# Up projections of three feed-forward layers as seven block products in place of eight, in a one-core backbone kernel

## The chip, the cores and the metric

The kernel runs on one core of a Trainium2 chip. The metric is device time in microseconds from start to end of one launch. The host lays data out, the core does all arithmetic. The engines are named as the profile names them: PE (TensorE, matmuls; PEld its weight loads), DVE (VectorE), ACT (ScalarE), POOL (GpSimd), SP (SyncE, which issues most transfers).

## The reference

A backbone of two layers works on 512 tokens (256 context, 256 latent) of width 1024. Each layer is: half-step SwiGLU, a token mixer, half-step SwiGLU; each is modulated by vectors of a conditioning product (w_ada) and wrapped in a LayerNorm.

```python
def swiglu(u, w_up, w_down):
    a, v = jnp.split(u @ w_up, 2, axis=-1)
    return (jax.nn.silu(a) * v) @ w_down

def ffn_sublayer(h, m, j, w_up, w_down, g, b):
    u = modulate(h, m[:, :, 3 * j], m[:, :, 3 * j + 1])
    return post_norm(h, swiglu(u, w_up, w_down), m[:, :, 3 * j + 2], FFN_RES_W, g, b)
```

w_up is 1024 x 5632 (gate half a, value half v), w_down 2816 x 1024. The latent tokens alone are the output, so the second layer's mixer and last feed-forward layer work on 256 columns; the three feed-forward layers before that point work on 512.

## The kernel before

Activations lie with features on the partitions and tokens along the row: u is 8 tiles of 128 x 512 (KT = 8), and half the columns (TL = 256) are context, half latent. All products are made of two parts: a number x is split into hi (x rounded to fp32r, by ACT) and lo (x - hi, by DVE), and `mm3` (L372 to L374) adds hi x hi, hi x lo and lo x hi into a PSUM bank. So each 128 x 128 weight block costs three matmuls.

Weights come in slots of eight blocks (128 x 1024, 512 KB), loaded by SP into one of three raw tiles (`wr`) in a fixed order, the plan. `split_ahead` makes wh (ACT, L342) and wl (DVE, L344) into one of three split slots, as far ahead of PE as slots are free. 

A feed-forward layer `ffn` has an up stage: for each of 22 feature tiles (`ft`), one bank gets the gate (eight blocks over kt), one the value; `act` applies SiLU on ACT (L760), multiplies with the value on DVE (L761), and splits the result into hi (L764) and lo (L765). The first pairs of tiles are begun together, column half by column half, while the LayerNorm of the layer before ends (`k_outer`); in the very first layer three pairs are begun in `ffn_start`. Then the down stage: eight output tiles `m` of 22 blocks each, the last two in column halves (`tail`). After each of them `res_tile` adds it to the residual and POOL sums it up for the LayerNorm (L595 to L599). In the down stage the tiles of u are free, and `more_slots` makes them into three further split slots.

Into both stages the kernel strews `ada_part`: a row block of the conditioning product that later layers need. It loads 128 x 1024 weights through the same raw tiles and makes, on DVE, a multiply-and-sum over 1024 for each of two vectors (L488, twice), then adds a bias (L492).

```python
raw = self.raw_next((("adb", l, j, k),))
for b in range(2):
    nc.vector.scalar_tensor_tensor(self.ada_scr, raw.rearrange("p a b -> p (a b)"), 1.0, self.sb[b],
                                   op0=ALU.mult, op1=ALU.mult, accum_out=o[:, b:b + 1])
```

The instructions on each engine stand in an order that a scheduler makes from the code's order when the kernel is built; each engine runs its own in that order.

## Time and profile before

| | |
|---|---|
| median of 3 runs | 2720.38 us (2718.14 to 2722.66) |
| the profiled execution, its own time | 2722.64 us |
| its span in the trace | 2720.7 us |
| PE busy | 2659.9 us, 98% |
| DVE / ACT / POOL busy | 71% / 45% / 13% |
| mean granted TensorE clock, as a share of full speed | 0.991 |

The busy time of an engine counts an instruction from its start to its end; those of PE overlap, so their pace is read from starts. What the engines do by stage is read from stretches of the trace.

### The profile page before, as it was taken

The page shows a single profiled execution, that of the slowest core. Times are in us where ns is not written, and L with a number is a line of the kernel's source. Part 1 is how long each engine was busy: PE and PEld are TensorE (multiplying, and loading weights), DVE is VectorE, ACT ScalarE, POOL GpSimd, SP SyncE. Part 2 cuts the span into 40 slices and gives each one's busy share as a digit, 9 for nine tenths or more (in the row PEclk, how much of TensorE's full clock was granted, in tenths as well). Part 3 has the DMA queues.
Part 4 walks back from the last instruction along what each step waited for, and adds up shares of the span by engine and source line. Part 5 has one row for each costly group of instructions (what it writes and reads, how often), then busy time and mean ns, then how long its engine had stood idle before and what let it go on. Part 6 is the DMA issues. An engine that isn't in the chain of part 4 may idle for free.

```text
span 2720.7 us, 38673 instructions
## 1 busy us (share of the span) xinstructions
PE 2659.9 (98%) x14869; PEld 2280.2 (84%) x14869; DVE 1928.3 (71%) x3469; ACT 1222.9 (45%) x1755; POOL 353.8 (13%) x296
## 2 busy tenths in 40 slices
PE   9999999999999999999999999999998999999998
PEld 7888897778887888888888888888977898899997
DVE  5788769599877545468887588633697998676654
ACT  4323237963345344433323142332388745574543
POOL 0000132112121000040000130001312112012002
PEclk9999999999999999999999999999999999999999
DMA  7666534134343222235666446532333354343563
GB/s 280 193 189 200 172 122 130 60 99 149 105 134 109 78 86 78 88 99 170 194 195 191 132 129 199 169 120 97 108 123 105 111 174 150 107 142 124 175 191 116
DMA packets 117833, 380.49 MB, mean 140 GB/s; under 512 B 13888, under 2 KB 22352, under 8 KB 117648
## 3 DMA queue, kind: packets, MB, share of 16 engines
q1 hardware_dynamic: 116000, 373.52, 42.5%
q0 software_dynamic: 1504, 4.34, 0.5%
q8 instruction: 116, 1.90, 0.3%
q14 instruction: 69, 0.57, 0.1%
q10 hardware_dynamic: 144, 0.17, 0.0%
HBM read 373.63 MB, written 4.33 MB: 139 GB/s over the span
## 4 chain that ended last, share of the span: by engine, by line
PE 56%; DVE 7%; ACT 3%; issue 2%; DMA 1%; POOL 0%; SPq 0%; POOLq 0%; DVEq 0%; ACTq 0%
PE bank L372 17%; PE bank L373 17%; PE bank L374 17%; PE bank L1282 1%; PE bank L1262 1%; DVE wl L344 1%; DVE x L869 1%; DMA wr<-in_ws_dram 1%; DMA x<-acs_d 1%; DVE f L669 0%; DVE m1l L344 0%; ACT wh L342 0%; PE bank L921 0%; DVE f L670 0%; DVE f L676 0%
## 5 line engine op out<-in xcount | busy, mean ns | idle before, releaser
L342 ACT ACTIVATE wh<-wr 128x1024 fp32r<-128x1024 f32 x388 | 410.2, 1058 | 727.1 <-PE bank L373 493.2
L344 DVE TENSOR_TENSOR wl<-wr,wh 128x1024 fp32r<-128x1024 f32 x388 | 483.6, 1247 | 239.4 <-ACT wh L342 237.6
L488 DVE SCALAR_TENSOR_TENSOR ada_scr<-wr,sb 128x1024 f32<-128x1024 f32 x256 | 316.7, 1237 | 135.9 <-DMA wr<-in_ws_dram 133.2
L372 PE MATMUL bank<-u0h,wh 128*128 128x512 f32 (+1 forms) x660 | 247.1, 376 | 5.5 <-ACT u0h L675 3.8
L372 PE MATMUL bank<-r,wh 128*128 128x512 f32 (+1 forms) x736 | 251.3, 342 | 0.0
L374 PE MATMUL bank<-r,wl 128*128 128x512 f32 (+1 forms) x736 | 249.9, 340 | 0.0
L373 PE MATMUL bank<-r,wh 128*128 128x512 f32 (+1 forms) x736 | 249.7, 340 | 0.0
L374 PE MATMUL bank<-u0h,wl 128*128 128x512 f32 (+1 forms) x660 | 237.2, 360 | 3.9 <-DVE wl L344 3.9
L373 PE MATMUL bank<-u0l,wh 128*128 128x512 f32 (+1 forms) x660 | 236.2, 358 | 2.1 <-DVE u0l L677 2.0
L373 PE MATMUL bank<-u1l,wh 128*128 128x512 f32 (+1 forms) x660 | 235.1, 357 | 0.8 <-DVE u1l L677 0.7
L372 PE MATMUL bank<-u1h,wh 128*128 128x512 f32 (+1 forms) x660 | 233.5, 356 | 0.6 <-ACT u1h L675 0.6
L374 PE MATMUL bank<-u1h,wl 128*128 128x512 f32 (+1 forms) x660 | 234.0, 355 | 0.0
L372 PE MATMUL bank<-u2h,wh 128*128 128x512 f32 (+1 forms) x660 | 233.6, 355 | 0.0
L374 PE MATMUL bank<-u2h,wl 128*128 128x512 f32 (+1 forms) x660 | 233.4, 354 | 0.0
L373 PE MATMUL bank<-u2l,wh 128*128 128x512 f32 (+1 forms) x660 | 233.2, 354 | 0.0
L373 PE MATMUL bank<-u3l,wh 128*128 128x512 f32 (+1 forms) x644 | 228.6, 355 | 1.5 <-DVE u3l L677 1.5
L372 PE MATMUL bank<-u3h,wh 128*128 128x512 f32 (+1 forms) x644 | 228.3, 356 | 0.0
L374 PE MATMUL bank<-u3h,wl 128*128 128x512 f32 (+1 forms) x644 | 228.0, 354 | 0.0
L372 PEld LDWEIGHTS bank<-r,wh 128*128 128x128 f32 x736 | 139.4, 190 | 15.3 <-issue 0.3
L374 PEld LDWEIGHTS bank<-r,wl 128*128 128x128 f32 x736 | 139.5, 190 | 15.1
L373 PEld LDWEIGHTS bank<-r,wh 128*128 128x128 f32 x736 | 139.5, 190 | 14.8
L372 PEld LDWEIGHTS bank<-u0h,wh 128*128 128x128 f32 x660 | 125.6, 191 | 29.7 <-issue 5.6
(530 smaller groups left out, 5919.4 us busy)
## 6 DMA issues: line engine op xcount, KB each, us to landing
wr<-in_ws_dram SPq DMA_DIRECT2D x602, 512.0 KB, 4.0
m1r<-in_ws_dram SPq DMA_DIRECT2D x29, 512.0 KB, 3.9
ada<-in_ws_dram SPq DMA_DIRECT2D x16, 512.0 KB, 9.0
x<-acs_d SPq DMA_DIRECT2D x22, 256.0 KB, 3.4
x<-acs_d SPq DMA_DIRECT2D x39, 128.0 KB, 3.6
x<-in_lw_dram SPq DMA_DIRECT2D x16, 256.0 KB, 3.2
f<-acs_d SPq DMA_DIRECT2D x25, 128.0 KB, 3.4
sb<-s_d SPq DMA_DIRECT2D x6, 512.0 KB, 5.8
```

The source lines that it names most:

```text
L342: self.pin(nc.scalar.activation(hi, raw, AF.Copy))
L344: self.pin(nc.vector.tensor_tensor(lo, raw, hi, op=ALU.subtract))
L372: x = self.pin(nc.tensor.matmul(out, st[0], mv[0], start=start, stop=False, skip_group_check=True))
L373: self.pin(nc.tensor.matmul(out, st[0], mv[1], start=False, stop=False, skip_group_check=True))
L374: self.last_mm = self.pin(nc.tensor.matmul(out, st[1], mv[0], start=False, stop=stop, skip_group_check=True))
L488: nc.vector.scalar_tensor_tensor(self.ada_scr, raw.rearrange("p a b -> p (a b)"), 1.0, self.sb[b], op0=ALU.mult, op1=ALU.mult, accum_out=o ...
L869: nc.vector.scalar_tensor_tensor(ys[:, :, a:z], xs[:, :, a + o:z + o], w(k), ys[:, :, a:z], op0=ALU.mult, op1=ALU.add)
L1262: nc.tensor.matmul(ps[:, 0:256], cc(kt[d], a), vv(a), start=True, stop=True)
L1282: nc.tensor.matmul(cc(po[w], c), lh, rh, start=n == 0, stop=n == len(steps) - 1, skip_group_check=True)
```

## The change

In the three layers with 512 columns, all feature tiles but the first four (five in the first layer) have their gate and value tile computed as one 2 x 2 by 2 x 2 product of quadrants. The weights' quadrants are a11, a12 (the gate's even and odd blocks over kt) and a21, a22 (the value's); the columns' are b11, b12 (even blocks of u, left and right half) and b21, b22 (odd blocks). `products` gives the order of the seven products of a tile p; each is four blocks of 128 x 128 on 256 columns, three matmuls a block. The slots of a tile's seven weight parts are half split slots, so that six parts fit.

- ACT and DVE split each part of 512 on its own (L451, L452) in place of a slot of 1024 at once. The parts of products 7, 6, 5 and 3 are sums of quadrants that POOL makes in place in the raw tiles or in a page (L420).
- `columns` makes the column sums on DVE and splits them, right after the first pairs; `columns_last` replaces one quadrant of u by another sum after the last unchanged tile.
- The outputs are put together from PSUM by copies (ACT) and additions (DVE, L517 to L521). From the ninth tile on v x g stays unsplit (L1027); `late_parts` splits it in the first block of the down stage, into the tiles of the column parts and of u, two results at a time; `move` has POOL copy 16 of these out of u again (L1057, L1061) before u becomes split slots.
- `ada_part(shared=True)` does one of the two sums as a product on POOL (L707), in place, and a sum on ACT (L708). There are two ada parts at a time in the first layer's unchanged tiles, one shared part in each changed tile, and four in a down block where there were two.
- A fourth raw tile is there in the up stage. LayerNorm's preparation moves from the start of the down stage to its sixth block.

```diff
+def products(n):
+    r = []
+    for p in range(n):
+        r += [(p, 1), (p, 7)] + ([(p - 1, 3)] if p else [])
+        r += [(p, m) for m in ((6, 4, 2, 5) if p < n - 1 else (6, 4, 5, 2, 3))]
+    return r
...
+        while len(self.sparts) < len(self.sops):
+            t = self.part_get()
+            if t is None:
+                return False
+            p, m = self.sops[len(self.sparts)]
+            R = self.sraw
+            if m in (1, 7):
+                n = i + 2 * p + (m == 7)
+                R[p, m] = self.raw_next(tuple(self.wlist[8 * n:8 * n + 8])), len(self.seq) - 1
...
+            if m == 1:
+                src = a11
+            elif m == 7:
+                R[p, 5] = self.F()
+                sub(R[p, 5], a21, a22, ALU.add)
+                sub(a21, a11, a21)
+                src = a21
+            elif m == 6:
+                sub(a11, R[p, 5], a11)
+                src = a11
+            elif m == 2:
+                src = a12
+            elif m == 4:
+                src = a22
+            else:
+                src = R[p, m]
+            nc.scalar.activation(flat(t.hi), src, AF.Copy)
+            nc.vector.tensor_tensor(flat(t.lo), src, flat(t.hi), op=ALU.subtract)
+            if m == 2:
+                R[p, 3] = self.F()
+                sub(R[p, 3], a12, a11)
+                self.raw_done(R[p, 1][1])
+            elif m == 4:
+                self.raw_done(R[p, 7][1])
+            elif m in (3, 5):
+                self.fF(src)
+            self.sparts.append(t)
+        self.wn += 2 * self.secs[i]
+        self.raw_less()
+        return True
...
+        for c, (p, m) in enumerate(products(n)):
...
+            X, Z, G, V = x_of[p][:, left], z_of[p], g_of[p], v_of[p]
+            out = Z[:, left] if m in (7, 4) else Z[:, right] if m == 2 else X
+            for b in range(4):
+                if m in (1, 2, 3):
+                    k, s = (2 * b + (m > 1), right if m == 3 else left)
+                    mv = self.uh[k][:, s], self.ul[k][:, s]
+                elif m == 4:
+                    mv = self.uh[2 * b][:, right], self.ul[2 * b][:, right]
+                else:
+                    mv = [x[:, b] for x in self.tparts[{5: 0, 6: 1, 7: 2}[m]]]
+                y = self.mm3(out, (t.hi[:, b], t.lo[:, b]), mv, m in (1, 7) and b == 0, b == 3)
...
+            if m == 1:
+                nc.scalar.activation(G[:, left], X, AF.Copy)
+            elif m == 7:
+                nc.scalar.activation(V[:, right], Z[:, left], AF.Copy)
+            elif m == 6:
+                nc.scalar.activation(V[:, left], X, AF.Copy)
+            elif m == 5:
+                nc.vector.tensor_tensor(V[:, right], X, V[:, right], op=ALU.add)
+            elif m == 4:
+                nc.vector.tensor_tensor(V[:, left], Z[:, left], V[:, left], op=ALU.add)
+            elif m == 2:
+                nc.vector.tensor_tensor(G[:, left], Z[:, right], G[:, left], op=ALU.add)
+                nc.scalar.activation(G[:, left], G[:, left], AF.Silu)
+                self.fB(Z)
+            elif m == 3:
+                nc.scalar.activation(G[:, right], X, AF.Silu)
+                self.fB(x_of[p])
+                finish(fts[p], G, V)
+                self.fF(G, V)
...
+        left, right = HALF
+        b11, b12 = self.ucol[:, :, 0, left], self.ucol[:, :, 0, right]
+        b21, b22 = self.ucol[:, :, 1, left], self.ucol[:, :, 1, right]
+        for o, a, b in ((b11, b12, b11), (b12, b22, b12), (b22, b22, b11), (b21, b21, b22)):
+            nc.vector.tensor_tensor(o, a, b, op=ALU.subtract)
...
+        for n, src in ((2, b12), (1, b22), (0, b11)):
+            hi, lo = self.tparts[n]
+            nc.scalar.activation(hi, src, AF.Copy)
+            nc.vector.tensor_tensor(lo, src, hi, op=ALU.subtract)
...
+        for b in range(KT // 2):
+            src, hi, lo = (x[:, s] for x, s in ((self.ucol[:, b, 1], HALF[0]), (self.uh[2 * b], HALF[1]),
+                                                (self.ul[2 * b], HALF[1])))
+            nc.scalar.activation(hi, src, AF.Copy)
+            nc.vector.tensor_tensor(lo, src, hi, op=ALU.subtract)
...
         nc = self.nc
         for l, j, k in self.ada_q[:n]:
             raw = self.raw_next((("adb", l, j, k),))
             o = self.mods[l][:, j, k, :]
-            for b in range(2):
-                nc.vector.scalar_tensor_tensor(self.ada_scr, raw.rearrange("p a b -> p (a b)"), 1.0, self.sb[b],
-                                               op0=ALU.mult, op1=ALU.mult, accum_out=o[:, b:b + 1])
+            r = raw.rearrange("p a b -> p (a b)")
+            for b in range(1 if shared else 2):
+                nc.vector.scalar_tensor_tensor(self.ada_scr, r, 1.0, self.sb[b], op0=ALU.mult, op1=ALU.mult,
+                                               accum_out=o[:, b:b + 1])
+            if shared:
+                nc.gpsimd.tensor_tensor(r, r, self.sb[1], op=ALU.mult)
+                nc.scalar.activation(r, r, AF.Copy, accum_out=o[:, 1:2])
             self.raw_done()
             c = PR["b_ada"] + j * KT + k
             nc.vector.tensor_scalar(o, o, self.par[l][:, c:c + 1], None, op0=ALU.add)
...
+        reg = 4 + (ps is not None) if paired else NFT
+        sums = ps is not None
+        self.with_u = paired
         ps = ps or self.ffn_begin(l, j, c0)
+        self.with_u = False
...
-        for ft in range(len(ps) // 2, NFT):
+        if paired:
+            self.columns(sums)
+        for ft in range(len(ps) // 2, reg):
             pp = [self.B(), self.B()]
             for i in range(2):
                 for kt in range(KT):
                     w = self.W(("up", l, j, kt, i * NFT + ft))
                     if kt == KT // 2:
-                        self.ada_part()
+                        self.ada_part(1 + sums)
                     self.mm3(pp[i][:, c0:], w, (self.uh[kt][:, c0:], self.ul[kt][:, c0:]), kt == 0, kt == KT - 1)
             act(*pp)
...
+        late = []
+        if paired:
+            self.columns_last()
+            def finish(ft, g, v):
+                if ft < NFULL:
+                    nc.vector.tensor_tensor(g, v, g, op=ALU.mult)
+                    hi, lo = self.R(), self.R()
+                    nc.scalar.activation(hi, g, AF.Copy)
+                    nc.vector.tensor_tensor(lo, g, hi, op=ALU.subtract)
+                    hid.append((hi, lo))
+                else:
+                    nc.vector.tensor_tensor(pages[ft - NFULL], v, g, op=ALU.mult)
+                    hid.append(None)
+                    late.append(ft)
+            def between(p, m):
+                if m == 4:
+                    self.ada_part(shared=True)
+            self.strassen(l, j, range(reg, NFT), finish, between)
...
+        def late_parts(n):
+            for ft in late[:n]:
+                src = pages[ft - NFULL]
+                hi, lo = his.pop(0) if his else spare.pop(0), spare.pop(0)
+                nc.scalar.activation(hi, src, AF.Copy)
+                nc.vector.tensor_tensor(lo, src, hi, op=ALU.subtract)
+                hid[ft] = hi, lo
+            del late[:n]
...
+            for ft in range(NFULL, NFT):
+                if ft >= NFT - 2:
+                    hi = q.tile([P, T], F32R, name=f"hh{l}{jm}_{ft}")
+                    nc.gpsimd.tensor_scalar(hi, hid[ft][0], 1.0, None, op0=ALU.mult)
+                else:
+                    hi = hid[ft][0]
+                lo = q.tile([P, T], F32R, name=f"hl{l}{jm}_{ft}")
+                nc.gpsimd.tensor_scalar(lo, hid[ft][1], 1.0, None, op0=ALU.mult)
+                hid[ft] = hi, lo
...
         for m in range(KT - TAIL):
             po = self.B()
+            if m == KT - TAIL - 1:
+                self.ln_prep()
             for ft in range(NFT):
                 w = self.W(("down", l, j, ft, m))
-                if ft in (8, 16):
-                    self.ada_part()
+                if late:
+                    late_parts(2)
+                if ft in (8, 16) or m and ft == 3 or (m or sums) and ft == 12:
+                    self.ada_part(shared=ft != 8)
                 if m == 1 and ft == 6:
                     self.res_mean(halves)
                 self.mm3(po[:, c0:], w, (hid[ft][0][:, c0:], hid[ft][1][:, c0:]), ft == 0, ft == NFT - 1)
+            if m == 0 and paired:
+                move()
+                more()
             self.res_tile(m, po, halves)
```

On DVE, at the place of one tile in the middle of the first layer's up stage. `wl` is a weight slot's low part, `ada_scr` an ada part's scratch, `f` a page, `r00` a result's part, `mods` the conditioning rows. Before:

```order
L344 TENSOR_TENSOR wl1_96<-wr0_90,wh1_95 128x1024
L488 SCALAR_TENSOR_TENSOR ada_scr_643,mods0_65<-wr1_91,sb0_641 128x1024
L488 SCALAR_TENSOR_TENSOR ada_scr_643,mods0_65<-wr1_91,sb1_642 128x1024
L492 TENSOR_SCALAR mods0_65<-mods0_65,par0_63 128x2
L488 SCALAR_TENSOR_TENSOR ada_scr_643,mods0_65<-wr0_90,sb0_641 128x1024
L761 TENSOR_TENSOR f13_112<-bank5_121,f13_112 128x512
L344 TENSOR_TENSOR wl2_98<-wr2_92,wh2_97 128x1024
L765 TENSOR_TENSOR r00_11_608<-f13_112,r00_10_607 128x512
L488 SCALAR_TENSOR_TENSOR ada_scr_643,mods0_65<-wr0_90,sb1_642 128x1024
L492 TENSOR_SCALAR mods0_65<-mods0_65,par0_63 128x2
```

Now, one changed tile late in the same stage (`uc00` is a page of v x g):

```order
L704 SCALAR_TENSOR_TENSOR ada_scr_621,mods0_65<-wr0_90,sb0_619 128x1024
L1027 TENSOR_TENSOR uc00_627<-f9_108,f8_107 128x512
L452 TENSOR_TENSOR wl2_98<-wr2_92,wh2_97 128x512
L452 TENSOR_TENSOR wl0_94<-f10_109,wh0_93 128x512
L519 TENSOR_TENSOR f12_111<-bank1_117,f12_111 128x256
L711 TENSOR_SCALAR mods0_65<-mods0_65,par0_63 128x2
L452 TENSOR_TENSOR wl0_94<-x00r0_634,wh0_93 128x512
L521 TENSOR_TENSOR f13_112<-bank1_117,f13_112 128x256
L452 TENSOR_TENSOR wl1_96<-wr2_92,wh1_95 128x512
L517 TENSOR_TENSOR f12_111<-bank0_116,f12_111 128x256
L452 TENSOR_TENSOR wl1_96<-x00r0_634,wh1_95 128x512
L452 TENSOR_TENSOR wl2_98<-f11_110,wh2_97 128x512
```

Two slots of 1024 and four passes over ada weights have become seven low parts of 512 (the seventh stands next, `wl2_98<-wr1_91`), one ada pass, one product and three additions from PSUM.

On POOL, for the same tile, where in this stage nothing stood before (`wr` and `x00r0` are raw tiles, here with the tile's gate and value weights; `sb1` is a vector of the conditioning). Now:

```order
L420 TENSOR_TENSOR f11_110<-wr2_92 128x512
L420 TENSOR_TENSOR wr2_92<-x00r0_634,wr2_92 128x512
L420 TENSOR_TENSOR x00r0_634<-f11_110,x00r0_634 128x512
L707 TENSOR_TENSOR wr0_90<-wr0_90,sb1_620 128x1024
L420 TENSOR_TENSOR f8_107<-x00r0_634 128x512
```

In place of none, POOL has four sums of 512 and one product of 1024 for each tile: the first sum is the part of product 5, the second that of 7, the third that of 6, the last that of 3.

On ACT, the same changed tile as on DVE (`wh` is a slot's high part, L511 to L515 copies out of PSUM, L522 and L525 the SiLU):

```order
L451 ACTIVATE wh2_97<-wr2_92 128x512
L525 ACTIVATE f8_107<-bank7_123 128x256
L451 ACTIVATE wh0_93<-f10_109 128x512
L515 ACTIVATE f12_111<-bank0_116 128x256
L708 ACTIVATE wr0_90,mods0_65<-wr0_90 128x1024
L451 ACTIVATE wh0_93<-x00r0_634 128x512
L451 ACTIVATE wh1_95<-wr2_92 128x512
L522 ACTIVATE f13_112<-f13_112 128x256
L451 ACTIVATE wh1_95<-x00r0_634 128x512
L451 ACTIVATE wh2_97<-f11_110 128x512
```

Where before one high part of 1024 stood between L760 and L764, the sum of the ada product (L708), which waits for POOL's L707, now stands ahead of the high part of product 6 (the row behind it) and of all that follow.

On DVE, in the first layer, between the fourth low part and the fifth (L560 is `columns_last`, L985 the low part of the last unchanged tile's result); before, such rows alternated with weight splits:

```order
L704 SCALAR_TENSOR_TENSOR ada_scr_621,mods0_65<-wr0_90,sb0_619 128x1024
L985 TENSOR_TENSOR r00_9_606<-f13_112,r00_8_605 128x512
L704 SCALAR_TENSOR_TENSOR ada_scr_621,mods0_65<-wr0_90,sb1_620 128x1024
L560 TENSOR_TENSOR u1l_85<-uc00_627,u1h_84 128x256
L711 TENSOR_SCALAR mods0_65<-mods0_65,par0_63 128x2
L704 SCALAR_TENSOR_TENSOR ada_scr_621,mods0_65<-wr2_92,sb0_619 128x1024
L560 TENSOR_TENSOR u2l_87<-uc00_627,u2h_86 128x256
L704 SCALAR_TENSOR_TENSOR ada_scr_621,mods0_65<-wr2_92,sb1_620 128x1024
L560 TENSOR_TENSOR u3l_89<-uc00_627,u3h_88 128x256
L711 TENSOR_SCALAR mods0_65<-mods0_65,par0_63 128x2
L704 SCALAR_TENSOR_TENSOR ada_scr_621,mods0_65<-wr0_90,sb0_619 128x1024
L452 TENSOR_TENSOR wl0_94<-wr1_91,wh0_93 128x512
```

Five passes of ada parts and three of the four small splits now stand ahead of the fifth low part, the last row; one more pass and that tile's product stand just before them, behind the fourth.

## Rows read from the trace of the kernel before

**Rows 1.** The page's part 1: busy us, share of the span and instructions.
```profile
PE 2659.9 (98%) x14869; PEld 2280.2 (84%) x14869; DVE 1928.3 (71%) x3469; ACT 1222.9 (45%) x1755; POOL 353.8 (13%) x296
```

**Rows 2.** Stretches: us, then busy us (instructions) by engine, PE clock, DMA.
```profile
62.00:268.00 206.00, 206.00 (x911) 170.57 (x910) 165.85 (x269) 62.00 (x77) 0.00 (x0) 1.00 0.62 193
268.00:346.00 78.00, 77.65 (x341) 63.65 (x340) 56.63 (x108) 20.80 (x24) 9.44 (x6) 1.00 0.53 169
1237.00:1455.00 218.00, 218.00 (x964) 180.50 (x963) 176.85 (x285) 67.30 (x85) 0.00 (x0) 1.00 0.61 195
```

**Rows 3.** PE in order of time, down stage, 512 columns: start us, us.
```profile
300.04 0.39 PE L372 MATMUL bank<-r,wh 128*128 128x512 f32 x1
...
303.44 0.39 PE L372 MATMUL bank<-r,wh 128*128 128x512 f32 x1
```

**Rows 4.** PE in order of time, layer 1's last up stage, 256 columns.
```profile
2560.01 0.28 PE L372 MATMUL bank<-u0h,wh 128*128 128x256 f32 x1
...
2562.89 0.28 PE L372 MATMUL bank<-u0h,wh 128*128 128x256 f32 x1
```

**Rows 5.** DVE in order of time, mixer, operations of 512.
```profile
450.87 0.69 DVE L946 SCALAR_TENSOR_TENSOR x<-x,x 128x512 f32<-128x512 f32 x1
451.47 0.68 DVE L955 TENSOR_TENSOR x<-x,x 128x512 f32<-128x512 f32 x1
```

**Rows 6.** DVE in order of time: one ada part, and the split after it.
```profile
318.03 1.23 DVE L488 SCALAR_TENSOR_TENSOR ada_scr<-wr,sb 128x1024 f32<-128x1024 f32 x1 [2.64 <-DMA wr<-in_ws_dram]
319.18 0.08 DVE L488 DVE_READ_ACCUMULATOR ada_scr<-wr,sb 128x1 f32 x1
...
320.70 1.22 DVE L344 TENSOR_TENSOR u2l<-wr,u2h 128x1024 fp32r<-128x1024 f32 x1
```

**Rows 7.** POOL in order of time, down stage: sums of 512 and 256.
```profile
300.86 2.26 POOL L599 TENSOR_TENSOR f<-f,f 128x512 f32<-128x512 f32 x1
...
348.33 2.27 POOL L599 TENSOR_TENSOR f<-f,f 128x512 f32<-128x512 f32 x1
...
360.82 1.29 POOL L597 TENSOR_TENSOR f<-f,f 128x512 f32<-128x512 f32 x1 [10.22 <-DVE f L560]
362.07 1.29 POOL L599 TENSOR_TENSOR f<-f,f 128x512 f32<-128x512 f32 x1
364.55 0.73 POOL L597 TENSOR_TENSOR f<-f,f 128x256 f32<-128x256 f32 x1 [1.19 <-DVE f L560]
365.24 0.73 POOL L599 TENSOR_TENSOR f<-f,f 128x256 f32<-128x256 f32 x1
```

**Rows 8.** DVE in order of time, beside the first two of rows 7.
```profile
300.69 1.29 DVE L488 SCALAR_TENSOR_TENSOR ada_scr<-wr,sb 128x1024 f32<-128x1024 f32 x1 [1.27 <-DMA wr<-in_ws_dram]
...
302.02 2.18 DVE L488 SCALAR_TENSOR_TENSOR ada_scr<-wr,sb 128x1024 f32<-128x1024 f32 x1
...
349.39 2.30 DVE L344 TENSOR_TENSOR wl<-wr,wh 128x1024 fp32r<-128x1024 f32 x1
351.61 1.21 DVE L488 SCALAR_TENSOR_TENSOR ada_scr<-wr,sb 128x1024 f32<-128x1024 f32 x1
```

**Rows 9.** Groups on ACT: shapes xcount | busy us, mean ns | idle before.
```profile
L342 ACT ACTIVATE wh<-wr 128x1024 fp32r<-128x1024 f32 x388 | 410.2, 1058 | 727.1 <-PE bank L373 493.2 <-issue 110.4 <-DMA wr<-in_ws_dram 93.6
...
L764 ACT ACTIVATE r<-f 128x512 fp32r<-128x512 f32 x66 | 41.4, 632 | 110.0 <-DVE f L761 110.0
...
L760 ACT ACTIVATE f<-bank 128x256 f32<-128x256 f32 x22 | 8.0, 369 | 0.0
```

**Rows 10.** POOL in order of time: one tensor with scalars, 256 columns.
```profile
392.94 0.55 POOL L681 TENSOR_SCALAR f<-f,par 128x256 f32<-128x256 f32 x1 [3.76 <-DVE f L670]
```

**Rows 11.** Stretches of 1 us in the mixer, columns as in rows 2.
```profile
505.00:506.00 1.00, 0.50 (x1) 0.19 (x1) 1.00 (x1) 1.00 (x3) 0.00 (x0) 1.00 0.00 0
...
507.00:508.00 1.00, 1.00 (x4) 0.80 (x3) 1.00 (x3) 1.00 (x1) 0.00 (x0) 0.50 0.86 205
```

More of the change, by code (lines that the diff above doesn't have):

```diff
@@ L105, in __init__, with sections @@
         self.wlist = wlist
+    @staticmethod
+    def sections(wlist):
+        r, last = {}, None
+        for i in range(len(wlist) // 8):
+            w = wlist[8 * i:8 * i + 8]
+            key = w[0][:3] if w[0][0] == "up" and tuple(x[3] for x in w) == KSPLIT else None
+            if key is None or key != last:
+                begin = i
+            if key is not None:
+                r[begin] = (i - begin + 1) // 2
+            last = key
+        return r
     def alloc(self, ctx):
@@ L328, in split_ahead @@
                 self.retire()
+            if i in self.secs:
+                if not self.strassen_parts(i):
+                    break
+                continue
             if not self.spl_free:
@@ new lines, in columns @@
+    def columns(self, sums):
+        nc = self.nc
+        if sums:
+            for i in range(KT // 2):
+                h, o = self.up[i]
+                nc.vector.tensor_tensor(self.ucol[:, i], h, o, op=ALU.add)
+        left, right = HALF
+        b11, b12 = self.ucol[:, :, 0, left], self.ucol[:, :, 0, right]
+        b21, b22 = self.ucol[:, :, 1, left], self.ucol[:, :, 1, right]
+        for o, a, b in ((b11, b12, b11), (b12, b22, b12), (b22, b22, b11), (b21, b21, b22)):
+            nc.vector.tensor_tensor(o, a, b, op=ALU.subtract)
+        self.tparts = [[x if self.dry else x.rearrange("p a (b c) -> p (a b) c", c=TL) for x in t] for t in self.tp]
+        for n, src in ((2, b12), (1, b22), (0, b11)):
+            hi, lo = self.tparts[n]
+            nc.scalar.activation(hi, src, AF.Copy)
+            nc.vector.tensor_tensor(lo, src, hi, op=ALU.subtract)
@@ L663, in ln_apply @@
         tp = self.F(keep=True)
-        up = self.F(keep=True) if nxt else None
+        up = self.F(keep=True) if nxt and not self.with_u else None
         for k in (2 * q, 2 * q + 1):
@@ L683, in ln_apply @@
                 nc.sync.dma_start(out[:, k], h)
[L684 removed]
+        self.fF(tp, *([up] if up is not None else []))
         if (i, q) == LAG[-1]:
@@ L785, in ffn, with more @@
+        def more():
+            x = [self.pair(p) for p in self.up[1:]]
+            self.more_slots([], x)
+            self.ring = [x[2], x[1]] + self.base + [x[0]]
+        self.res_begin(l, jm, 0.5, c0, prep=False)
+        if not paired:
+            more()
         self.set_cuts(c0)
@@ L1621, in run @@
                         with tc.tile_pool(name=f"ffn{l}{j}", bufs=1, reuse_waits="tile") as rp:
-                            self.rpages = [rp.tile([P, T], F32R, name=f"r{l}{j}_{i}") for i in range(2 * NFT)]
+                            n = 2 * (NFT if c0 else NFULL)
+                            self.rpages = [rp.tile([P, T], F32R, name=f"r{l}{j}_{i}") for i in range(n)]
+                            if not c0:
+                                self.tp = [[rp.tile([P, 2, T], F32R, name=f"t{l}{j}{i}{h}") for h in "hl"]
+                                           for i in range(3)]
                             self.ada_begin(rp)
```

112 lines of the change are left out of this document (98 added, 14 removed).

## The prediction

> **What bounds the kernel now.** I read the page first. Its busy shares put PE at 98% and POOL at 13% [rows 1]: PE is the engine on which the end hangs, and POOL has little to do. Then I took the stretches that the change touches, each apart. In both up stretches PE is busy all of the time, in the down stretch all but 0.4 us, at a granted clock of 1.00; DVE is busy 81% of an up stretch, and POOL not at all [rows 2]. So an up stage costs what its matmuls cost, DVE has a fifth of the time to spare, and POOL's 0.00 says that nothing there has yet been tried against DVE.
>
> The pace of a matmul is read from starts, since the durations overlap. On 512 columns, 15 matmuls lie between the two rows shown: 3.40 / 15 = 0.2267 us [rows 3]. On 256 columns, 24 lie between: 2.88 / 24 = 0.120 us [rows 4]. Half the columns cost 53% of the time.
>
> **PE, what is saved.** A feature tile (gate and value) was 2 x 8 blocks x 3 matmuls = 48 x 0.2267 = 10.88 us. It becomes 7 products x 4 blocks x 3 = 84 matmuls on 256 columns, 84 x 0.120 = 10.08 us. So 0.80 us a tile, 7.4%, not an eighth. 17 tiles of the first feed-forward layer and 18 of the next two (the third with c0 = 0 is layer 1's first) go this way: 53 x 0.80 = **42 us**, if PE stays the bound. The Trainium skill (TensorE: Matmul & The Clock Gate, Back-to-back issue gap) puts a warm start-to-start gap at N / 2.4 ns plus 2.5, so 109 ns for 256 columns and 216 for 512; by that an estimate of the saving would be 53 x (48 x 0.216 - 84 x 0.109) = 64 us. The rows are slower than that at both sizes, and they decide.
>
> **DVE and POOL, what is added.** Before, a tile took two weight splits and two modulation rows (an ada part: two multiply-and-sum passes of 1024 on DVE) and no POOL. Now the order shows, per tile: on DVE seven low parts of 512, one product v x g of 512, one ada pass of 1024, three additions that read PSUM; on POOL four sums of 512 and one product of 1024 (L420, L707).
>
> These two engines do not run side by side. At 300.86 a POOL sum took 2.26 us, where the undisturbed one takes 1.29 [rows 7]: it waited for the DVE pass that began at 300.69. The next DVE pass, at 302.02, took 2.18, not 1.23 [rows 8, 6]. At 348.33 the same: POOL 2.27, and DVE 2.30 where the form takes 1.2 [rows 7, 8]. One POOL sum of 512 thus costs DVE 0.95 (2.18 - 1.23) to 1.08 us (2.30 - 1.22); its own pace undisturbed is 1.25 (362.07 - 360.82) and that of 256 is 0.69 [rows 7]. I take 1.1 for 512. The product of 1024 is in no row: each 256 more cost 0.56, so 1.25 + 1.12 = 2.37 undisturbed, 2.2 less the same 0.15.
> The Trainium skill (SBUF — State Buffer, Who interferes with whom) says that a DVE instruction with two SBUF inputs and a GpSimd instruction that reads SBUF exclude each other for the whole instruction, and that one with a single SBUF input does not. The trace agrees on the first (the four rows above); by the second the three PSUM additions stay outside the sum, which no row here isolates.
>
> DVE's paces: 0.60 for 512 from start to start [rows 5], 1.15 for one pass of 1024, 2.67 for a whole unshared ada part [rows 6]. So a tile's time on what DVE and POOL share is
> - DVE 8 x 0.60 + 1.15 = 5.95
> - POOL 4 x 1.1 + 2.2 = 6.6
> - together **12.55 us**, above PE's 10.08 and above the old 10.88.
>
> To this comes time in which neither runs, from ACT's place in the chain. In ACT's order the sum of the ada product (L708, 1024 long, at least the 1.06 of a cast of that length) stands ahead of the cast of the sixth product's part. So after POOL's 1024 product come 1.06 + 0.63 of ACT [rows 9], during which POOL has one sum of 1.1 to do: 0.6 idle. Then the casts for the parts of products 2, 5 and the next 1 follow a SiLU of some 0.37 (the row of L760 on 256), each 0.63 against DVE's 0.60 [rows 9, 5]: some 0.8 more. I take **14.0 us a tile**; the bounds are 12.55 (all of it hidden) and 15.6 (POOL at 1.25 and 2.37, DVE at its full durations 0.69 and 1.23, that is 7.4 + 6.75, and 1.5 idle). PE then waits some 4 us in each tile; its six parts of look-ahead cover nothing, since the shortage lasts. The 11 tiles below the eighth also split their result on the spot, 0.60 each. Sum: 53 x (14.0 - 10.88) + 11 x 0.60 = **+172 us** (bounds +95 and +257).
>
> **Ahead of the first product.** In the first layer DVE has to do, between the end of the first three tiles on PE and the first runs of parts: eight ada parts less one pass (8 x 2.67 - 1.3 = 20.1), seven column operations of 1024 (8.0), five results (5 x 1.2), two weight splits (2.3), four small splits (1.4): 37.8 us, against two tiles of PE, 21.8. The order puts six of the ada passes between the fourth part and the fifth. Stall 16 us. In the other two layers: four ada parts 10.7, columns 8.0, results 4.8, splits 3.4 and 1.4, 28.3 us against 21.8 + 2.9 of PE: 4 us each. Together **+24 us** (10 to 35). Before, the same ada parts lay in DVE's spare fifth [rows 2].
>
> **Down stage.** In blocks 0 and 1 (PE 2 x 66 x 0.2267 = 29.9 us) the shared pair of engines has: 14 late splits (8.4), six weight splits (6.8), seven ada parts, two of them unshared (4.6) and five shared at 1.15 + 2.2 (16.7), 16 POOL copies of 512 (0.55 for 256 [rows 10], so about 1.0), the residual's two sums and eight rescalings (7.0). That is 59.5 us, a lag of 30. Three weight slots of look-ahead (3 x 24 x 0.2267 = 16.3) swallow part, 14 us remain; from block 2 on the three more slots carry the rest. Three layers: **+40 us** (0, if copies and ada parts fall into gaps, to 100, if each of the blocks 2 to 5 also runs over). Block 1 reads the copied low parts; that is where PE would stand.
>
> **Sum.** -42 is contained in the tile price. 172 + 24 + 40 = +236 against the profiled execution's own 2722.6: 2958.6; the median of the runs shown is 2.3 lower, so **2956 us**.
>
> What costs nothing: the weights' bytes are the same, and 3 loads a tile where there were 4 over a shorter time; ACT's work per tile grows to some 8 us, under 14, so only its order counts; the removed page for u and the earlier column form lie in the normalisation, where DVE does the same instructions into another tile.
>
> **Rivals.**
> 1. *PE stays the bound* (the other side). If DVE and POOL overlapped, the tile would cost 10.08, and only the 24 us of DVE work ahead of the products stand against 42: 2722.6 - 18 - 2.3 = 2702 us. It decides as soon as the pair's sum falls under 10.88, that is if POOL's five instructions cost DVE under 4.9 us and not 6.6. For it: POOL's rows are few, and none stands beside the 512 low parts of this form. Against: both collisions shown lost about a whole POOL instruction. Chance 0.06.
> 2. *The pair is packed without gaps*, and the down stage hides its lag: +95 + 10 + 0, 2825 us. For it: other work of POOL can fill ACT's time. Chance 0.13.
> 3. *The clock falls too.* In one microsecond with PE busy 0.50 the granted clock is still 1.00, soon after it is 0.50, half of 2.4 GHz [rows 11]. With PE at 72% (10.08 / 14.0) of a tile and in pieces, stretches at 1.2 GHz are likely; a tile wholly there would take at most 84 x 0.24 = 20.2. If half the time is spent there, 15.1: +58, 3014 us. Against: parts then pile up and PE regains the ground at full clock. Chance 0.12.
> 4. *Within 0.2%*: the terms cancel. Nothing points there; 0.02.
>
> My forecast (12.9 to 15 a tile) has 0.67. Cases faster by over 0.2%, about what a measurement of this kernel can tell from no change: 0.06; within: 0.02; slower: 0.92. The range for 8 in 10 takes in most of rivals 2 and 3: 2830 to 3070.
>
> **What the changed profile would show.** Right, if in the up stretches PE falls to some 72 to 80%, its waits end with DVE's low parts (L452) and behind them POOL L420 and ACT L451; if POOL's sums of 512 last well over 1.29 and DVE's low parts over 0.69, so that both seem busy nearly all the time; if 7 x 12 matmuls take about 14 us. Step two is right if, in the first layer, PE stands some 10 us before the fifth part. Step three, if PE waits in block 1 for POOL's copies L1061 or for weight splits behind them. I am wrong if DVE's low parts keep 0.60 beside a running POOL sum, or if PE is above 95% there: then the mechanism failed, not a size. If the tiles take 12.6, only my idle time was wrong; if PE's clock is under 0.9 over whole tiles, rival 3 has joined.

## The result and the profile after

The changed kernel takes **3199.32 us** (median of 4 runs, 3197.59 to 3201.34), the one before 2719.93: a ratio of 1.1762, with a 95% interval of 1.1741 to 1.1782. It is 479 us slower. The forecast was 236 slower, within 2830 to 3070: the direction was right, the size half of what came.

The page's part 1, to be held against [rows 1]: PE is down from 98% to 87% of a longer span, POOL up from 354 to 1042 us.

```profile
PE 2769.4 (87%) x16777; PEld 2447.5 (77%) x16777; DVE 2339.9 (73%) x3738; ACT 1497.9 (47%) x2445; POOL 1041.8 (33%) x652
```

Stretches of the first layer (us; then busy us and instructions of PE, PEld, DVE, ACT, POOL; granted clock; DMA share; GB/s). The first is its up stage, the second its down stage, the third ten tiles late in the up stage, 17.6 us each. In [rows 2] PE was busy all of the time, at a clock of 1.00.

```profile
62.00:376.50 314.50, 227.41 (x1495) 214.35 (x1494) 256.12 (x303) 128.56 (x260) 156.34 (x85) 0.85 0.31 103
376.50:562.00 185.50, 134.50 (x643) 113.76 (x643) 109.32 (x181) 57.19 (x86) 96.48 (x49) 0.83 0.36 128
191.60:367.90 176.30, 123.91 (x842) 119.83 (x841) 135.91 (x146) 68.30 (x140) 94.31 (x50) 0.84 0.28 92
```

**Where the time went.** I measured each stage from PE's first and last matmul on `r`, the split results, that is a down stage's first and (all but a few matmuls) last work. The first layer's pair, before and after:

```profile
264.52 0.39 PE L372 MATMUL bank<-r,wh 128*128 128x512 f32 x1
...
389.89 0.28 PE L374 MATMUL bank<-r,u3l 128*128 128x256 f32 x1
```

```profile
376.56 0.40 PE L586 MATMUL bank<-r,wh 128*128 128x512 f32 x1
...
561.81 0.28 PE L588 MATMUL bank<-r,u2l 128*128 128x256 f32 x1
```

So the down stage starts 112.0 us later, and takes 185.3 us where it took 125.4. The same rows in the other two layers, and in the runs below, give this table (us against the kernel before; up is the sum of three stages, with what lies ahead of the products; the tile is read from the start of one product 7 to the next, over the last ten tiles of the first layer or a part of them). In the changed kernel the other 11 of the 475 us by which its span is longer lie behind the down stages.

| kernel | time | up | down | a tile |
|---|---|---|---|---|
| forecast | 2956 | +196 | +40 | 14.0 |
| changed kernel | 3199 | +332 | +132 | 17.6 |
| two pages for product 5's sum | 3171 | +309 | +130 | 16.7 |
| product 2 in its own bank | 3081 | +219 | +126 | 14.2 |
| own bank and two pages | 3079 | +217 | +127 | 14.0 |
| parts unshared in the down stages | 3109 | +335 | +39 | 17.7 |
| parts unshared everywhere | 2977 | +209 | +38 | 14.6 |
| own bank, parts unshared | 2933 | +168 | +31 | 13.2 |
| own bank, no POOL in the up stages | 2811 | +28 | +51 | 10.7 |
| own bank, POOL with four idle sums a tile | 2988 | +181 | +76 | 14.0 |
| own bank, POOL with four idle copies a tile | 2904 | +98 | +77 | 12.3 |
| own bank, POOL with four idle fills a tile | 2815 | +26 | +56 | 10.7 |
| own bank, no POOL, without the four sums | 2753 | -14 | +35 | 10.1 |

**One tile of the changed kernel**, POOL and DVE in order of time (start us, us, and in brackets the idle time before and what ended it). Product 7 of this tile starts on PE at 208.66, that of the next at 225.97.

```profile
210.24 1.29 POOL L420 TENSOR_TENSOR f<-wr 128x512 f32<-128x512 f32 x1 [7.45 <-DVE wl L452]
211.60 1.62 POOL L420 TENSOR_TENSOR wr<-wr,wr 128x512 f32<-128x512 f32 x1
213.30 2.13 POOL L420 TENSOR_TENSOR wr<-f,wr 128x512 f32<-128x512 f32 x1
215.40 2.79 POOL L707 TENSOR_TENSOR wr<-wr,sb 128x1024 f32<-128x1024 f32 x1
218.15 1.71 POOL L420 TENSOR_TENSOR f<-wr 128x512 f32<-128x512 f32 x1
```

```profile
210.89 1.18 DVE L452 TENSOR_TENSOR wl<-wr,wh 128x512 fp32r<-128x512 f32 x1 [0.73 <-ACT wh L451]
212.00 2.31 DVE L704 SCALAR_TENSOR_TENSOR ada_scr<-wr,sb 128x1024 f32<-128x1024 f32 x1
214.24 0.08 DVE L704 DVE_READ_ACCUMULATOR ada_scr<-wr,sb 128x1 f32 x1
214.24 1.75 DVE L1027 TENSOR_TENSOR hr<-f,f 128x512 f32<-128x512 f32 x1
215.91 2.82 DVE L452 TENSOR_TENSOR wl<-wr,wh 128x512 fp32r<-128x512 f32 x1
218.66 1.75 DVE L452 TENSOR_TENSOR wl<-f,wh 128x512 fp32r<-128x512 f32 x1
220.33 0.41 DVE L519 TENSOR_TENSOR f<-bank,f 128x256 f32<-128x256 f32 x1
```

In this tile no DVE pass with two SBUF inputs keeps its pace beside POOL: 1.18, 1.75 and 2.82 us where 0.69 is the undisturbed duration of 512, 2.31 where it is 1.23 for 1024 [rows 5, 6]. Five such passes take 9.8 us, ahead of L519. And L519 is what PE waits for (48.1 us in ten tiles, 10 times):

```profile
215.01 0.39 PE L586 MATMUL bank<-t000h,wh 128*128 128x256 f32 x1 [0.43 <-ACT f L515]
...
220.80 0.58 PE L586 MATMUL bank<-u0h,wh 128*128 128x256 f32 x1 [4.94 <-DVE f L519]
...
223.94 0.28 PE L587 MATMUL bank<-t000l,wh 128*128 128x256 f32 x1
...
225.97 0.28 PE L586 MATMUL bank<-t002h,wh 128*128 128x256 f32 x1
```

That wait is in no step of the forecast. L519 adds product 4 to the value tile; it reads the bank Z into whose other half product 2 is written next. So PE stands 4.9 us at product 2, though that part has long been split; meanwhile no slot comes free, ACT and DVE run out of parts to split, and POOL stands 7.45 us. In these 17.31 us, by their rows, neither DVE nor POOL runs for 3.2; over ten tiles one of the two runs 14.2 us of 17.6. Behind the stand PE's clock is at half (columns as in the stretches above):

```profile
220.80:223.94 3.14, 3.14 (x14) 3.14 (x15) 0.85 (x3) 0.39 (x1) 0.00 (x0) 0.50 0.38 146
```

**The down stage**, first layer: DVE, then ACT, POOL and PE in order of time.

```profile
396.17 0.08 DVE L704 DVE_READ_ACCUMULATOR ada_scr<-wr,sb 128x1 f32 x1
411.28 0.26 DVE L711 TENSOR_SCALAR mods<-mods,par 128x2 f32<-128x2 f32 x1 [15.04 <-ACT wr L708]
411.42 0.48 DVE L780 SCALAR_TENSOR_TENSOR f<-bank,gp,f 128x256 f32<-128x256 f32 x1
```

```profile
410.10 1.06 ACT L708 ACTIVATE wr<-wr 128x1024 f32<-128x1024 f32 x1 [16.27 <-POOL wr L707]
...
436.50 1.06 ACT L708 ACTIVATE wr<-wr 128x1024 f32<-128x1024 f32 x1 [10.46 <-POOL wr L707]
...
437.55 1.04 ACT L391 ACTIVATE wh<-wr 128x1024 fp32r<-128x1024 f32 x1
```

```profile
404.82 2.94 POOL L1061 TENSOR_SCALAR hl<-u2l 128x512 fp32r<-128x512 f32 x2
407.73 2.33 POOL L707 TENSOR_TENSOR wr<-wr,sb 128x1024 f32<-128x1024 f32 x1
410.04 1.48 POOL L1057 TENSOR_SCALAR hh<-u3h 128x512 fp32r<-128x512 f32 x1
```

```profile
411.95 2.08 PE L792 MATMUL bank<-f,ones 128*128 128x512 f32 x2 [14.65 <-DVE f L780]
...
438.65 0.79 PE L586 MATMUL bank<-t002l,wh 128*128 128x512 f32 x1 [15.91 <-ACT wh L391]
```

Read from the end: PE waits 14.65 us for L780; L780 stands on DVE behind L711, an addition to two columns; L711 waits 15.04 us for ACT's sum, that for POOL's product L707, and that stands behind POOL's copies. DVE does nothing in that time. The second stand, 15.91 us, is the same on ACT: the split L391 that PE needs is queued behind a sum L708 that waits for POOL.

### The profile page after: what moved, and what is told of

Its sections match the earlier page's. It is cut to its first block, busy times and chain, and to the rows that moved or that the text cites. A ratio compares the mean times of both kernels' runs of the same rounds, so it can differ in the third digit from the quotient of the medians.

```text
span 3195.9 us, 44747 instructions
## 1 busy us (share of the span) xinstructions
PE 2769.4 (87%) x16777; PEld 2447.5 (77%) x16777; DVE 2339.9 (73%) x3738; ACT 1497.9 (47%) x2445; POOL 1041.8 (33%) x652
## 5 line engine op out<-in xcount | busy, mean ns | idle before, releaser
L391 ACT ACTIVATE wh<-wr 128x1024 fp32r<-128x1024 f32 x286 | 301.4, 1055 | 396.9 <-PE bank L587 217.1
L586 PE MATMUL bank<-u0h,wh 128*128 128x256 f32 (+1 forms) x660 | 239.1, 365 | 201.8 <-DVE f L519 192.1
L707 POOL TENSOR_TENSOR wr<-wr,sb 128x1024 f32<-128x1024 f32 x86 | 228.6, 2659 | 157.5 <-DVE ada_scr L704 150.4
L452 DVE TENSOR_TENSOR wl<-wr,wh 128x512 fp32r<-128x512 f32 x196 | 237.3, 1214 | 45.8 <-ACT wh L451 44.0
L451 ACT ACTIVATE wh<-wr 128x512 fp32r<-128x512 f32 x196 | 122.4, 628 | 269.0 <-PE bank L587 122.1
L708 ACT ACTIVATE wr<-wr 128x1024 f32<-128x1024 f32 x86 | 91.0, 1058 | 328.4 <-POOL wr L707 328.4
L588 PE MATMUL bank<-u0h,wl 128*128 128x256 f32 (+1 forms) x660 | 221.7, 336 | 7.6 <-DVE wl L393 6.3
L587 PE MATMUL bank<-u0l,wh 128*128 128x256 f32 (+1 forms) x666 | 223.7, 336 | 2.3 <-DVE u0l L897 2.0
L587 PE MATMUL bank<-u1l,wh 128*128 128x256 f32 (+1 forms) x666 | 222.1, 334 | 3.3 <-DVE u1l L897 2.4
L420 POOL TENSOR_TENSOR f<-wr 128x512 f32<-128x512 f32 x80 | 119.1, 1489 | 322.6 <-DVE wl L452 238.1
L587 PE MATMUL bank<-u2l,wh 128*128 128x256 f32 (+1 forms) x666 | 220.8, 332 | 1.7 <-DVE u2l L560 1.0
L586 PE MATMUL bank<-u2h,wh 128*128 128x256 f32 (+1 forms) x660 | 218.3, 332 | 0.8 <-ACT u2h L895 0.8
L588 PE MATMUL bank<-u1h,wl 128*128 128x256 f32 (+1 forms) x660 | 218.5, 332 | 0.0
L586 PE MATMUL bank<-u1h,wh 128*128 128x256 f32 (+1 forms) x660 | 218.0, 333 | 0.4 <-ACT u1h L895 0.4
```

The costliest lines, as they stand in the source:

```text
L391: self.pin(nc.scalar.activation(hi, raw, AF.Copy))
L420: sub = lambda o, a, b, op=ALU.subtract: nc.gpsimd.tensor_tensor(o, a, b, op=op)
L451: nc.scalar.activation(flat(t.hi), src, AF.Copy)
L452: nc.vector.tensor_tensor(flat(t.lo), src, flat(t.hi), op=ALU.subtract)
L586: x = self.pin(nc.tensor.matmul(out, st[0], mv[0], start=start, stop=False, skip_group_check=True))
L587: self.pin(nc.tensor.matmul(out, st[0], mv[1], start=False, stop=False, skip_group_check=True))
```

## The experiments

All are edits of the changed kernel. Each time is that of one run, but for the second and third run of 5, which are medians of four; the runs of one kernel lie within 6 us of each other. Theory A to D are named in the expectations; B is the forecast's own view, that only the sum of the work which DVE and POOL share counts.

**1. Two pages for the sum of product 5.**

```diff
-                R[p, 5] = self.F()
+                R[p, 5] = self.rst[(64, 128)[p % 2]]
...
```

> The sum for product 5 gets two pages of its own in turn (the two constant pages of the mixers, set again after each up stage); nothing else changes. Theory A, a closed round: in the changed kernel POOL stands 7.45 us in each tile until DVE has split product 5's part, since the next tile's first sum writes the page that this split reads. With two pages the first two sums of a tile (1.3 and 1.6 us) are done in that time, and the round of 17.1 us loses about 2.9: tile 14.2, time 3199 - 53 x 2.9 = about 3045. Theory B, the sum of what DVE and POOL share is the limit (as forecast): their work is the same, so 3199 within 25. Theory C, the addition L519 in DVE's queue, on which product 2 waits, sets the round: no gain either, 3199 within 25.

3171.32 us, 28 less, 0.9 a tile: A's 154 did not come, and the 25 that B and C allow are missed by 3. POOL's first sum, which now writes a page of its own (named rst), waits for the load of the value tile or for ACT instead (the first two rows of POOL's waits over seven tiles: us in all, times, longest).

```profile
POOL rst L420 <- DMA wr<-in_ws_dram: 29.1, 6, 5.7
POOL rst L420 <- ACT wh L451: 8.8, 2, 4.4
```

So POOL's 7.45 us were for the most part what the round left over, not what made it; that part of theory A fell.

**2. Product 2 in a bank of its own, alone and with the pages.**

```diff
-            out = Z[:, left] if m in (7, 4) else Z[:, right] if m == 2 else X
+            out = Z[:, left] if m in (7, 4) else Y[:, right] if m == 2 else X
...
```

> Product 2 gets a PSUM bank of its own, so that it no longer waits for the addition of product 4 (L519), which reads the bank that both shared and stands in DVE's queue behind the product's split that waits for POOL. Theory A (closed round): PE's 4.9 us wait takes in product 2 and the next tile's product 1 (1.4 us each), slots come free as much earlier, and the round loses up to 2.9: about 3045; with a little more if the clock stays up. Theory B (sum of the shared work): PE waits the same, only elsewhere (at product 7 for its split): 3199 within 25. Theory C (this wait alone sets the round): 4.9 a tile, 3199 - 53 x 4.9 = 2940.

> Both edits, the bank for product 2 and the two pages for the sum of product 5. Theory A: the two gains add up as far as the shared work allows: tile 17.1 - 5.8 = 11.3, held up by the 12.55 to 14.0 of DVE's and POOL's shared work, so about 13, and 3199 - 53 x 4.1 = about 2980. Theory B: 3199 within 25. Theory C: as with the bank alone, 2940.

3080.73 and 3078.62 us: the bank gives 119 us, nearest to A's 154, and the pages nothing more (A's 2980 for both is missed). B's 3199 and C's 2940 are further off. PE's wait for the addition is gone, and in the run with the bank alone seven tiles take 99.4 us, 14.2 each:

```profile
226.50:325.90 99.40, 82.41 (x591) 80.82 (x590) 87.04 (x102) 46.07 (x99) 60.51 (x35) 0.88 0.34 112
```

By their rows, DVE or POOL now runs in 97.1 of these 99.4 us, and the tile is at about the forecast's 14.0. That fits the shared pair as the limit, but does not show it: PE still does not wait for low parts, only for ACT's copy of product 6 (L511 of this run), which stands in ACT's queue behind the sum that waits for POOL's product. These are PE's only wait and ACT's longest in these seven tiles (us in all, times, longest):

```profile
PE bank L582 <- ACT f L511: 16.8, 7, 3.3
ACT wr L704 <- POOL wr L703: 18.9, 7, 3.0
```

With the pages too, DVE or POOL runs in 92.2 of the same 99.4 us, and the tile is as long.

**3. Modulation parts whole on DVE, everywhere and in the down stages alone.**

```diff
-                    self.ada_part(shared=True)
+                    self.ada_part()
...
-                    self.ada_part(shared=ft != 8)
+                    self.ada_part()
```

> Every modulation part is done whole on DVE again (both passes), so that POOL's product of 1024 and ACT's sum of it are gone from the up and the down stages; POOL keeps the four sums and the copies. In the down stages DVE stood 15.0 us in the first layer at the small addition L711, which waits for ACT's sum, and that for POOL's product behind 16 copies. Theory D (the head of the queue): the down stages lose most of their 150 us, some 110; in a tile the product's 2.8 us are gone from the round and DVE's second pass of 1.15 comes in: 17.1 - 1.7 = 15.4, 90 us; together about 3000. Theory B (sums of shared work): each part is cheaper by 2.2 - 1.15 = 1.05; 53 + 3 x 7 parts x 1.05 = 78 us, about 3120.

> The changed kernel with the modulation parts of the down stages alone done whole on DVE; the up stages keep their shared parts, so their tiles stay at 17.4 us. Theory D (heads of queues: DVE stands at the small addition L711 until POOL has got through its copies to the product and ACT has summed it): the down stages fall as in the run with all parts unshared, from 185 to 140, 169 to 139 and 153 to 134 us, together 94, and the time to about 3105. Theory B (sums of shared work): seven parts a layer at 2.2 - 1.15 = 1.05 less each, 22 us, 3177. Rival (the down stage is late because the up stage ahead of it left splits and loads behind): no change, 3199 within 15.

2976.74 and 3108.55 us (the second is the second hunk alone). Theory D's 3000 and 3105 are met within 23 and 4 us, B's 3120 and 3177 are 143 and 68 off. The down stages fall by 94 and 93 us; the up stages move only in the first run. In the first layer's down stage PE's waits (us in all, times, longest) are now:

```profile
PE bank L586 <- ACT wh L391: 8.3, 1, 8.3
PE bank L843 <- POOL f L817: 4.5, 1, 4.5
PE bank L792 <- DVE f L780: 1.9, 1, 1.9
```

**4. Bank apart and parts unshared.** The two diffs above together.

> Product 2 in its own bank and unshared modulation parts, the sums still on POOL. If the two gains are separate causes they add: 3199 - 119 - 223 = 2857. If the shared work of DVE and POOL is the limit once the bank is apart: per tile DVE 8 x 0.60 + 2 x 1.15 = 7.1 and POOL 4 x 1.1 = 4.4, 11.5, plus up to 1 idle: tile 12.0, 2977 - 53 x (15 - 12) = 2818.

2932.85 us, tile 13.2: both missed. The gains (119 and 223) do not add, since both shorten the same tile. What keeps it 1.2 over the 12.0 of the second was not taken further; PE's main wait there is for the addition of product 5 on DVE, 9.0 us in five late tiles.

**5. No POOL in the up stages**, without and with the bank, and with copies on ACT (the first hunk with those of 3; the second in the last of the three runs alone).

```diff
-        sub = lambda o, a, b, op=ALU.subtract: nc.gpsimd.tensor_tensor(o, a, b, op=op)
+        sub = lambda o, a, b, op=ALU.subtract: nc.vector.tensor_tensor(o, a, b, op=op)
...
-                    nc.gpsimd.tensor_scalar(hi, hid[ft][0], 1.0, None, op0=ALU.mult)
+                    nc.scalar.activation(hi, hid[ft][0], AF.Copy)
...
-                nc.gpsimd.tensor_scalar(lo, hid[ft][1], 1.0, None, op0=ALU.mult)
+                if ft % 2:
+                    nc.scalar.activation(lo, hid[ft][1], AF.Copy)
+                else:
+                    nc.gpsimd.tensor_scalar(lo, hid[ft][1], 1.0, None, op0=ALU.mult)
```

> The four sums of a tile go to DVE and the modulation parts are whole on DVE: POOL does nothing in the up stages (its copies ahead of the down stage stay). Per tile DVE then has 12 passes of 512 at 0.60, two of 1024 at 1.15 with their small ones (0.25), three additions from PSUM at 0.35: 10.8, as long as the old tile of 10.88. Theory A (the wait for POOL behind L519 made the round): the tile falls from 17.4 to about 11 to 12, the down stages stay at 140 us as in the run with unshared parts, and the time is 2720 + 3 x 15 + 53 x (0.1 to 1.1) + 15 ahead of the products = 2785 to 2840. Rival: the seven products are slow on PE itself (half clock, more weight loads) or ACT's splits hold them: then the tile stays over 13, and the time over 2890.

> As the run without POOL in the up stages, with product 2 in a bank of its own. Theory A: with short passes in DVE's queue the addition L519 is late by no more than 1 to 2 us, so the bank is worth 0 to 1 us a tile: 2785, at most 55 less than the run without it. Rival, the wait for the bank is independent of POOL: it is worth the same 3 us a tile as before, 160 us.

> As the run with the bank apart and no POOL in the up stages, and in addition nine of the sixteen copies ahead of the second down block (those of odd feature tiles and the two high parts) on ACT and the other seven on POOL. If POOL's copies at 1.48 each are what is left of the loss in the down stage (140 against 125 us before), it falls by about 10 us in each of the three layers: 30 us under that run, about 2755. If it is the splits and the weights' buffers there, no change within 10.

2814.59 us, within theory A's 2785 to 2840; 2810.94 (ratio to the kernel before 1.033, 1.0313 to 1.0348); 2793.59 (1.0269, 1.0253 to 1.0284). The bank is worth 3.6 us here, no more than the runs of one kernel differ (2809.24 to 2812.69), and 119 with POOL: sharing it hurts where DVE's queue is slow. The copies gave 17 of the 30 expected, 16 of them in the down stages. Ten tiles of the second run, 10.7 each, with DVE busy in all but 0.04 of 107.2 us:

```profile
162.20:269.40 107.20, 106.10 (x842) 102.28 (x841) 107.16 (x201) 57.34 (x121) 0.00 (x0) 1.00 0.44 148
```

**6. POOL work for which nobody waits** until the stage ends, when DVE sets its page again; added to the second run of 5: four sums, four copies, or four fills a tile (one of the three lines).

```diff
...
+                        for _ in range(4):
+                            nc.gpsimd.tensor_tensor(t, o, o, op=ALU.add)
...
+                            nc.gpsimd.tensor_scalar(t, o, 1.0, None, op0=ALU.mult)
...
+                            nc.gpsimd.memset(t, 1.0)
...
```

> The run with the bank apart and no POOL in the up stages, and to it four POOL sums of 512 a tile, for which nobody waits: they add a constant page to itself into a second page (both set again after the stage), behind the tile's modulation part. Their only effect on the kernel is what they take from DVE by running. The forecast's price is 0.95 to 1.08 us of DVE for each: with DVE busy all of the 10.77 us of a tile, the tile becomes 14.6 to 15.1 and the time 2811 + 53 x 4 x 1.0 = about 3023. Rival (the loss came from waits for results and for buffers, and the engines overlap): tile 10.8, time 2811 within 15.

> As the run with four unused POOL sums a tile, but with POOL copies of one input in their place (the form of L1061, 1.48 us for 512). Ahead of the down stage such copies took 2.6 us each beside DVE's two-input passes, while those lasted 1.21 as ever. If it is so here, POOL is slowed and DVE is not: tile 10.8, time 2811 within 20. Rival: any POOL pass that reads SBUF costs DVE its length: tile 14.5 or more, time over 3000.

> As the run with four unused POOL sums a tile, but with four fills of 512 that read nothing. If the loss needs POOL to read SBUF: tile 10.8, time 2811 within 15. Rival (any work of POOL slows DVE): tile over 12, time over 2880.

2988.28, 2904.24 and 2815.12 us: 177, 93 and 4 more than 2810.94 (212 instructions of the kind added in each). DVE and POOL beside the sums:

```profile
222.37 1.49 DVE L452 TENSOR_TENSOR wl<-x00r,wh 128x512 fp32r<-128x512 f32 x1
223.78 1.52 DVE L420 TENSOR_TENSOR f<-x00r 128x512 f32<-128x512 f32 x1
225.23 1.52 DVE L452 TENSOR_TENSOR wl<-f,wh 128x512 fp32r<-128x512 f32 x1
226.68 1.52 DVE L452 TENSOR_TENSOR wl<-wr,wh 128x512 fp32r<-128x512 f32 x1
228.12 0.68 DVE L1027 TENSOR_TENSOR hr<-f,f 128x512 f32<-128x512 f32 x1
```

```profile
222.27 5.38 POOL L1039 TENSOR_TENSOR rst<-rst 128x512 f32<-128x512 f32 x4
```

and beside the copies:

```profile
220.28 1.07 DVE L452 TENSOR_TENSOR wl<-wr,wh 128x512 fp32r<-128x512 f32 x1
221.27 0.68 DVE L420 TENSOR_TENSOR f<-wr 128x512 f32<-128x512 f32 x1
221.87 1.09 DVE L452 TENSOR_TENSOR wl<-f,wh 128x512 fp32r<-128x512 f32 x1
222.89 0.68 DVE L452 TENSOR_TENSOR wl<-x00r,wh 128x512 fp32r<-128x512 f32 x1
```

Each sum costs one DVE pass 0.83 us (1.52 - 0.69); each copy 0.40, every other pass; the fills nothing (DVE stays at 0.69). The sums come near the price of 0.95 to 1.08 and rule out the rival's 2811 us; the copies missed both expectations. Over the last ten tiles of the first layer it is (13.99 - 10.72) / 4 = 0.82 and (12.28 - 10.72) / 4 = 0.39 us of time for each. The whole times hold more: some 25 us of the 177 and of the 93 lie in the down stages, where in the first layer DVE stands 3.3 and 5.2 us until the last of these sums or copies is done and it can set the page again.

**7. Without the four sums.** The second run of 5, with products 7 and 6 on raw quadrants and 5 and 3 on constant pages. It leaves the sums out, so what it computes is not the layer; it serves to read PE's own pace.

```diff
-                R[p, 5] = self.F()
-                sub(R[p, 5], a21, a22, ALU.add)
-                sub(a21, a11, a21)
+                R[p, 5] = self.rst[128]
...
-                sub(a11, R[p, 5], a11)
...
-                R[p, 3] = self.F()
-                sub(R[p, 3], a12, a11)
+                R[p, 3] = self.rst[64]
...
```

> The run with the bank apart and no POOL in the up stages, without the four sums of weights in a tile: products 7 and 6 take the raw quadrants, products 5 and 3 constant pages. All matmuls, splits and modulation parts stay. DVE then has 10.8 - 2.4 = 8.4 us a tile and PE 84 x 0.120 = 10.08. If PE's own saving is as forecast: tile 10.1, time 2811 - 53 x 0.69 = 2774, less what the first tiles gain. Rival (PE itself is slower on seven products, or another engine holds it): tile stays at 10.7 or more.

2753.41 us, and the tile of 10.1 that was expected if PE's saving is as priced. Ten tiles take 100.8 us with PE busy throughout, 10.08 each:

```profile
151.10:251.90 100.80, 100.80 (x842) 100.80 (x841) 85.10 (x162) 58.73 (x120) 0.00 (x0) 1.00 0.49 158
```

No version that computes everything came under 2720 us.

## Why the forecast was right in direction and wrong in size

- **PE's saving** is as priced: 84 matmuls take 10.08 us (experiment 7), 0.80 less than the old tile. An estimate by the formula of the Trainium skill (TensorE: Matmul & The Clock Gate, Back-to-back issue gap), which that section gives for the isolated gap of a single matmul, would put the tile at 84 x 0.109 = 9.2 us; experiment 7 decides for the row.
- **DVE and POOL slow each other**: shown by experiment 6, where nothing in the tile waits for POOL. The price was mis-sized: 0.83 us a sum, where I took 1.1 from pairs of 1024 and 512. The three additions from PSUM, which I put at nothing because they do not contend with POOL, are DVE time all the same (3 x 0.41 a tile, in series with its other passes; in the bank run of experiment 2 they last 0.41 beside POOL's instructions too), and experiment 5 shows it: 12 x 0.60 + 2 x 1.15 = 9.5 would be the sum without them, 10.7 was measured. The two errors cancel about. Even so it is in part luck that the forecast's 14.0 stands beside 14.2 in experiment 2: 14.0 was 12.55 of work and 1.45 in which neither runs, and in experiment 2 one of the two runs for 13.9 of the 14.2.
- **The step that failed** is "I take 14.0 us a tile": it counts work and ACT's order, and takes the shared pair to be never idle otherwise. In the changed kernel the tile was 17.6, since PE waits for L519 (forecast: waits that "end with DVE's low parts") through a bank that product 4's reader and product 2 share. A collision that lengthens five passes thus costs twice: once as work, once as PE's stand, in which the pair runs dry. Parting the bank takes 113 of the 332 us off the up stages; +219 is left, against 172 + 24 forecast. Over the late tiles PE's waits end with readers of PSUM in both kernels, and with low parts, as forecast, in neither.
- **Ahead of the first product**: forecast a stall of 16 us in the first layer. In the changed kernel the products begin at 81.3, and the first tile takes 27.1 us from product 7 to product 7 (82.7 to 109.8), 9.5 more than a late one. PE idles 10.9 us there in nine waits, the longest 4.1 us, for a low part. The sign holds; the size is some 10, where I took 16, and it is spread over the tile, not one stand at the fifth part.
- **Down stage**: forecast 40, measured 132. I priced the shared parts as work and asked how much of it PE's look-ahead covers. But each is a chain DVE, POOL, ACT, DVE, whose last link L711 stands in DVE's queue, and whose third stands in ACT's. Experiment 3 settles it: with the chain gone from the down stages alone, 93 of the 132 us come back (22 by the sum of the work), and 39 remain. The copies, priced at 1.0, took 1.48 and were a further cause: 16 of the 51 us in the second run of experiment 5 (its down stages are at +35 with the copies shared out; what makes up these 35 was not taken further).
- **Rival 3**, the clock: it did fall, to 0.84 over late tiles, with PE busy 70% of them (forecast 72 to 80%). In the tile above it is 0.50, that is 1.2 GHz, behind PE's stand: 14 matmuls take 3.14 us there, where 14 x 0.12 = 1.68 is their time at full clock. How much of these 1.5 us the changed kernel's tile keeps was not tried by itself. The two runs of experiment 2 have clocks of 0.88 and 0.93 in the same stretch and tiles of 14.1 and 14.0 us, so there it can count for little. (The forecast's 15.1 holds for half of the matmuls at 1.2 GHz; for half of the time it would be 10.08 / 0.75 = 13.4.)

The Trainium skill (SBUF — State Buffer, Who interferes with whom) also says that a GpSimd instruction which only writes SBUF does not contend with a DVE pass of two SBUF inputs: the fills agree (4 us in 2811). Where it has one block the other for the whole of an instruction, the rows differ: a sum of 1.35 us (5.38 / 4) took 0.83 from DVE, a copy of 1.6 took 0.40.

## What to carry to other kernels

A sum of work per engine gives the limit of a loop, not its time: before trusting it, look up for every PSUM bank and every small instruction what it waits for, and what stands behind it in its queue. Work handed to an idle engine and fetched back puts that engine's whole queue in front of the next instruction of both, so hand over only what nobody in the loop waits for. POOL's idle time is not free beside a DVE that is busy with two-input passes: a sum there took more from DVE than the same sum done on DVE (0.83 against 0.60 us).

## What was not expected of the hardware

- In the three forms tried, POOL's price to DVE goes by what POOL reads: 0.83 us for a sum of two inputs of 512, 0.40 for a copy of one, none for a fill; the DVE passes beside them lasted 1.52, 1.07 to 1.09 and 0.69 us.
- A copy of 512 on POOL took 1.48 us alone (L1057), more than a sum of two inputs at 1.29 [rows 7].
